# Delta-net trunk: when a background column is added up, where q's square sums are scaled, and what the values and decay products wait for

## The chip, the cores and the metric

The kernel runs on one core of a Trainium2 chip. Its engines work in parallel, each through its own instructions in order: TensorE (PE in the profile) multiplies matrices and transposes through an identity, VectorE (DVE) and ScalarE (ACT) work element by element, GpSimd (POOL) takes small work, SyncE (SP) issues DMAs. Engines wait for each other by semaphores. Matrix products land in PSUM, which this kernel cuts into named tiles of 128x512 floats: four called `acc`, two called `mm` and two called `sc`.

The metric is the device time of one execution, in microseconds (us). Three runs of the kernel before took 2936.68, 2944.91 and 2948.51 us; the median is 2944.91 us.

## The reference

A trunk of two layers over 1024 positions of width 1024. Each layer is a mixer and a gated feed-forward network, both modulated by six vectors per layer that are computed from a conditioning vector `c`. The mixer of layer 0 is a gated delta net with 8 heads, that of layer 1 is retention.

```python
e = jax.nn.silu(c @ cond_w + cond_b)
for i in range(DEPTH):
    mod = (e @ ada_w[i] + ada_b[i])[:, None, :]
    sh1, sc1, g1, sh2, sc2, g2 = jnp.split(mod, 6, axis=-1)
    y = mixers[i % N_MIXERS](x * (1.0 + sc1) + sh1)
    x = layer_norm(DN_ALPHA * x + (1.0 + g1) * y, ln_g[i, 0], ln_b[i, 0])
    y = conv_ffn(x * (1.0 + sc2) + sh2, ffn_up[i], ...)
    x = layer_norm(DN_ALPHA * x + (1.0 + g2) * y, ln_g[i, 1], ln_b[i, 1])
```

The delta net, cut to what the change touches:

```python
qkv = jax.nn.silu(causal_dwconv(qkv, conv_w))
q = _l2norm(q) * (dk ** -0.5)          # divides by sqrt(sum of squares + 1e-6)
k = _l2norm(k)
kk = jnp.where(strict, (k * beta) @ k.T * decay, 0.0)
...                                     # solve with (I + kk), scan over chunks
o = o * lax.rsqrt(jnp.mean(o * o, -1) + 1e-6) * norm_w
```

## The kernel before, in words

The stage that matters is the delta net, about 85 to 645 us of the span. The 8 heads go through it as 4 pairs, numbered 0 to 3. For each pair the kernel runs several Python generators: `t_path` (decay matrices and the inverse of a triangular matrix in 32x32 blocks), `t_chain` (the inverse put together from 32 to 64 to 128 by small matmuls), `prep` (values and keys transposed to PSUM and scaled back by VectorE), `dt_half` (products of keys and queries times the decay), and two `scan`s over 8 chunks with `tail`s that normalize the output. Beside them runs one generator `filler`: the projections of the normalized input onto q, k, v and z, some 30 units of 48 matmuls `acc<-hT` of 128x512 each. The function `run` interleaves all of them into one order for TensorE: it keeps an estimated clock (each matmul has a cost), takes the generator of the lowest priority number that is ready, and lets `filler` go on where nothing else is ready. A generator that yields a number sleeps so long on that clock; one that yields `after_ev(...)` waits for events that others emit, and `emit(name, lat)` sets an event that much after the clock. TensorE keeps exactly this order (`pm` and `ptr` pin each instruction behind the last). The orders of VectorE, ScalarE, GpSimd and the DMA queues are not pinned: a scheduler places each of their instructions from the program and its dependencies.

The steps that are touched, with the lines of the profile:

* **Square sums.** `ssq_tile` transposes a finished q feature to an `acc` tile (L717 `acc<-cst,qkv`), ScalarE squares it chunk by chunk with a running sum (L509), and one VectorE operation on 128x8 numbers adds 1e-6 and scales (L511). It is run once for each of the 8 q features, the first ones before the pairs start. The scaled sums are read only in `tail`, at L1090.
* **Features.** `conv_half` copies a projection out of `acc` (L485, L488), VectorE adds three shifted terms (L490), and ScalarE applies the silu (L491).
* **The 32x32 inverse.** Row by row on VectorE (L883, L885), then VectorE transposes it (L888, `RX`), ScalarE reorders it (L890), VectorE transposes that (L892, `TX`). `t_path` then emits `("Tq", p)` at once, and `("T", p)` 4.98 us later on the estimated clock. `t_chain` waits for `("T", p)`; ScalarE copies blocks of `TX` (L919, six of them) and `RX` (L930, eight) into place before its first matmuls `mm<-T,U`.
* **Values and decay products.** `prep` and `dt_half` wait for `("Tq", p)`. `prep` transposes values to an `mm` tile (L717 `mm<-cst,qkv`), VectorE scales them out of it (L994). `dt_half` multiplies keys and queries into an `mm` tile (L714 `mm<-qkv`), VectorE multiplies by the decay that a DMA has loaded (L1029). There are two `mm` tiles, so a third group on TensorE waits until VectorE has emptied the first.
* **Background columns.** The modulation vectors needed later are computed in the background: `bg_ada` puts 8 units per vector on a list `bg`, and every call of `bg_step` (one per unit of `filler`) takes the next one. A unit loads 256 rows of a matrix (SyncE's queue) and returns its work with a count, which goes on the list `pend` and is run that many calls later: VectorE multiplies and adds into the tile `ada` (L237, L239), of which there is one buffer. After four units TensorE transposes `ada` (L249), ScalarE copies the four blocks back into `ada` with row sums (L251), and VectorE adds the bias (L253, or L255 where no 1 is added). Three vectors, 24 units, are computed during the delta net; `filler` calls `bg_step` 29 times. More are computed in later stages.

TensorE's order around a pair's inverse is: filler matmuls, square sums, `mm<-qkv` and `mm<-cst,qkv` groups mixed with filler, then the 32x32 chain `mm<-T,U`, filler, the 64x64 chain, and the scan.

Of the kernel before, what the change touches and what calls it, by code (L numbers as in the profile page):

```python
# [33 lines left out]
def trunk_kernel(ctx: ExitStack, tc, A):  # L34
# [84 lines left out]
    def bg_step(tile=mm_tile):  # L119
        bg_ps[0] = tile  # L120
        for p in pend:
            p[0] -= 1
        while pend and (pend[0][0] <= 0 or not bg):
            pend.pop(0)[1]()
            if not bg:
                break
        if bg:
            nxt = bg.pop(0)()
            if nxt:
                pend.append(list(nxt))  # L130
# [90 lines left out]
    def bg_ada(i, j, kind):  # L221
# [8 lines left out]
        def work(nh, kp, wr):  # L230
# [3 lines left out]
            for kk in range(2):  # L234
                k = kp * 2 + kk
                if k == 0:
                    dve.tensor_scalar(a, wr[:, 0], e[:, 0:1], None, ALU.mult)  # L237
                else:
                    dve.scalar_tensor_tensor(a, wr[:, kk], e[:, k:k + 1], a, ALU.mult, ALU.add)  # L239
            if kp < KT // 2 - 1:  # L240
                return
            if kind == "col":
# [7 lines left out]
                for g in range(4):  # L250
                    act.activation(a[:, g * P:(g + 1) * P], tp[:, g * P:(g + 1) * P], AF.Copy, accum_out=pt[:, g:g + 1])  # L251
                if j in (1, 2, 4):
                    dve.scalar_tensor_tensor(v, pt, 1.0, b, ALU.add, ALU.add)  # L253
                else:
                    dve.tensor_add(v, pt, b)  # L255
            else:
# [240 lines left out]
    def ssq_tile(ti, tr):  # L497
        o = feats[ti]
        r = ssq[ti] = ct(f"ssq{ti}", [P, NCH])
        for half in range(2):  # L500
            pt = acc_tile()
            sq = tl("cv", [P, 516], name="sq")
            for c in range(4):
                cs = slice(c * P, (c + 1) * P)
                tr(pt[:, cs], o[half][:, cs])
            for c in range(4):
                n = half * 4 + c
                cs = slice(c * P, (c + 1) * P)
                act.activation(sq[:, cs], pt[:, cs], AF.Square, accum_out=r[:, n:n + 1])  # L509
        if ti < GH:  # L510
            dve.tensor_scalar(r, r, 1e-6, 1e-6 * P, ALU.add, ALU.mult)  # L511
        else:
            dve.tensor_scalar(r, r, 1e-6, None, ALU.add)

# [204 lines left out]
    def after_ev(*names):  # L719
        return ("ev", names)  # L720
# [265 lines left out]
    def prep(p):  # L986
        heads = pairs[p]
        yield after_ev(("Tq", p), *[("f", 2 * GH + h) for h in heads])
        for q4 in range(2):
# [17 lines left out]
    def dt_half(p, q4):  # L1007
        heads = pairs[p]
        if q4 == 0:
            yield after_ev(("Tq", p), ("M", p - 1))  # L1010
            yield from take("lane", 1)
            t = tl("lane", [P, 2, HALF], name="DT")
            tiles = [t[:, 0], t[:, 1]]
        else:
            yield after_ev(("Tq", p), ("S", p - 1))
            yield from take("auh", 2)
            emit(("Dt", p))
            tiles = [tl("auh", [P, HALF], name="DT") for _ in range(2)]
# [563 lines left out]

    def layer_tail(i, mix, wout, xsrc, x_mid, x_out, ln_next, final):
        sc2, sh2 = fold(i, 1, 2 * i)
        if i == 0:
# [75 lines left out]
        while rowq or rowp:  # L1661
# [4 lines left out]
                       (gb2, x_out) if final else None, ln_next, "hTb", ("hTb", "hTa", 8, 6, "f") if final else ("qkv", "hTa", 8, 4, "0"), x_out, ("out", i)))  # L1666

    g1 = two("auh", F32, "g1")
    for nh in range(2):
# [353 lines left out]
```

## Time and profile before

| | |
|---|---|
| runs | 2936.68, 2944.91, 2948.51 us; median 2944.91 us |
| the profiled execution: its time | 2944.47 us |
| its span, first to last instruction | 2942.7 us |
| mean granted TensorE clock | 0.983 |
| instructions | 38900 |
| DMA | 459.01 MB, mean 156 GB/s |

How to read the lines of the profile: `L994` is line 994 of the kernel. A line of a timeline has the start in us from the span's start, the length in us, the engine, the line, the operation, what it writes and reads (`out<-in`), the shape, and how many such instructions in a row it stands for; in brackets how long the engine had been idle before and which instruction of which engine it had waited for. Consecutive matmuls are pipelined, so their lengths overlap; the distance of two starts is what one costs. A line of a view of waits has: engine, its instruction, whom it waited for, and the idle time in total, the number of times and the longest in us. A line of a view of windows has the stretch, its length, the busy time of PE, PE's weight loads, DVE, ACT and POOL with instruction counts, the granted TensorE clock as a share of full speed, the DMA share and the rate. In a view of one line of code each row gives the shortest, median and longest duration in ns, and the first and last start.

### The profile page before, as it was taken

The page shows a single profiled execution, that of the slowest core. Times are in us where ns is not written, and L with a number is a line of the kernel's source. Part 1 is how long each engine was busy: PE and PEld are TensorE (multiplying, and loading weights), DVE is VectorE, ACT ScalarE, POOL GpSimd, SP SyncE. Part 2 cuts the span into 40 slices and gives each one's busy share as a digit, 9 for nine tenths or more (in the row PEclk, how much of TensorE's full clock was granted, in tenths as well). Part 3 has the DMA queues.
Part 4 walks back from the last instruction along what each step waited for, and adds up shares of the span by engine and source line. Part 5 has one row for each costly group of instructions (what it writes and reads, how often), then busy time and mean ns, then how long its engine had stood idle before and what let it go on. Part 6 is the DMA issues. An engine that isn't in the chain of part 4 may idle for free. (4 is left out here: it accounts for less than half of the span.)

```text
span 2942.7 us, 38900 instructions
## 1 busy us (share of the span) xinstructions
PE 2815.8 (96%) x13594; PEld 2298.3 (78%) x13594; DVE 2208.4 (75%) x3976; ACT 1314.9 (45%) x2413; POOL 497.8 (17%) x517
## 2 busy tenths in 40 slices
PE   8999899999999999999999999999999899999997
PEld 6887777887778888887778877777777788888886
DVE  6878788656688888868686665566689787777779
ACT  4745564444544444545333333222344544444543
POOL 0312221100013332200000021422202023331001
PEclk9999899999999999999999999999999999999999
DMA  7231222243255655755333364655663253334753
GB/s 279 80 119 62 80 79 80 83 167 137 93 176 175 208 189 188 270 185 184 132 136 115 129 231 145 208 171 170 194 231 131 102 165 133 135 126 162 291 184 115
DMA packets 248276, 459.01 MB, mean 156 GB/s; under 512 B 23632, under 2 KB 77264, under 8 KB 248080
## 3 DMA queue, kind: packets, MB, share of 16 engines
q1 hardware_dynamic: 215680, 404.87, 40.9%
q10 hardware_dynamic: 29760, 43.00, 4.0%
q0 software_dynamic: 2640, 8.65, 0.8%
q8 instruction: 107, 1.75, 0.2%
q14 instruction: 89, 0.73, 0.1%
HBM read 343.71 MB, written 112.72 MB: 155 GB/s over the span
## 5 line engine op out<-in xcount | busy, mean ns | idle before, releaser
L714 PE MATMUL acc<-hT,wh 128*128 128x512 f32 x960 | 301.3, 395 | 0.0
L1504 PE MATMUL acc<-bb,ab 128*128 128x512 f32 x984 | 236.2, 398 | 10.9 <-DVE bb L90 9.3
L1504 PEld LDWEIGHTS acc<-bb,ab 128*128 128x128 f32 x984 | 186.0, 191 | 55.2 <-DVE bb L90 14.2
L714 PEld LDWEIGHTS acc<-hT,wh 128*128 128x128 f32 x960 | 183.4, 191 | 34.5
L1229 PE MATMUL acc<-T,wb 128*128 128x512 f32 x840 | 203.6, 391 | 6.9 <-DVE wb L90 6.8
L89 ACT ACTIVATE ab<-ar 128x512 fp32r<-128x512 f32 x210 | 130.2, 626 | 171.2 <-PE mm L303 46.9
L714 PE MATMUL acc<-hT,wl 128*128 128x512 f32 x480 | 202.3, 421 | 0.0
L411 POOL TENSOR_TENSOR xg<-xg,gb 128x512 f32<-128x512 f32 x48 | 62.4, 1302 | 773.6 <-DMA xg<-xs 761.4
L1229 PEld LDWEIGHTS acc<-T,wb 128*128 128x128 f32 x840 | 156.5, 188 | 45.0 <-DVE wb L90 10.4
L90 DVE TENSOR_TENSOR ab<-ar,ab 128x512 fp32r<-128x512 f32 x210 | 147.5, 708 | 57.6 <-ACT ab L89 57.6
L90 DVE TENSOR_TENSOR wl<-wr,wh 128x1024 fp32r<-128x1024 f32 x98 | 123.0, 1256 | 86.9 <-ACT wh L89 86.7
L1654 POOL TENSOR_TENSOR o<-o 128x512 f32<-128x512 f32 x80 | 124.7, 1568 | 288.8 <-ACT pc L1290 190.1
L90 DVE TENSOR_TENSOR wb<-wr,wb 128x512 fp32r<-128x512 f32 x162 | 116.9, 726 | 71.6 <-ACT wb L89 69.4
L89 ACT ACTIVATE wh<-wr 128x1024 fp32r<-128x1024 f32 x98 | 103.9, 1062 | 143.5 <-PE acc L714 70.5
L90 DVE TENSOR_TENSOR wb<-mm,wb 128x512 fp32r<-128x512 f32 x216 | 145.8, 683 | 27.5 <-ACT wb L89 26.8
L1633 DVE SCALAR_TENSOR_TENSOR o<-g,vc,o 128x512 f32<-128x512 f32 (+2 forms) x176 | 155.0, 897 | 5.3 <-ACT o L1628 4.6
L89 ACT ACTIVATE wb<-mm 128x512 fp32r<-128x512 f32 x216 | 124.0, 595 | 64.4 <-DVE mm L1279 61.3
L1290 ACT ACTIVATE pc<-acc 128x512 f32<-128x512 f32 x143 | 84.6, 592 | 144.2 <-PE acc L1229 88.5
L89 ACT ACTIVATE wb<-wr 128x512 fp32r<-128x512 f32 x162 | 98.6, 627 | 107.6 <-DMA wr<-in_ffn_up 50.2
L714 PE MATMUL acc<-wh,hT 128*128 128x512 f32 x384 | 135.2, 416 | 1.0 <-DVE vv L90 1.0
L110 PE MATMUL acc<-T,wb 128*128 128x512 f32 x292 | 116.0, 397 | 9.4 <-DVE wb L90 9.4
L490 DVE SCALAR_TENSOR_TENSOR qkv<-raw,vc,qkv 128x512 f32<-128x512 f32 x144 | 110.3, 769 | 14.2 <-ACT qkv L488 13.5
(651 smaller groups left out, 7456.4 us busy)
## 6 DMA issues: line engine op xcount, KB each, us to landing
wr<-in_ffn_up SPq DMA_DIRECT2D x92, 512.0 KB, 4.3
mvw<-in_ada_w SPq DMA_DIRECT2D x80, 512.0 KB, 4.4
ad<-o SPq DMA_DIRECT2D x154, 256.0 KB, 3.1
ar<-ad SPq DMA_DIRECT2D x154, 256.0 KB, 3.8
Br<-in_ffn_down SPq DMA_DIRECT2D x88, 256.0 KB, 3.4
wr<-in_ret_wv SPq DMA_DIRECT2D x32, 512.0 KB, 4.2
ar<-od SPq DMA_DIRECT2D x56, 256.0 KB, 4.9
wr<-in_gdn_wqkv SPq DMA_DIRECT2D x24, 512.0 KB, 3.5
```

Source lines behind the costliest of these rows:

```text
L89: act.activation(dst_h, src, AF.Copy)
L90: eng.tensor_tensor(dst_l, src, dst_h, ALU.subtract)
L110: mm(acc, wl[:, k], hl[0], start=first, stop=False)
L411: pool.tensor_tensor(x, x, gb[0], ALU.mult)
L490: dve.scalar_tensor_tensor(oh, raw[:, 3 - j:515 - j], w[:, 3 - j:4 - j], oh, ALU.mult, ALU.add)
L714: pq(pe.matmul(out, lhsT, rhs, start=start, stop=stop), cost)
L1229: return pe.matmul(*a, skip_group_check=True, **kw)
L1290: act.activation(t, X, AF.Copy)
L1504: return pe.matmul(*args, skip_group_check=True, **kw)
L1633: dve.scalar_tensor_tensor(tv, gv[:, c0 - j:c1 - j], w[:, 2 - j:3 - j], tv, ALU.mult, ALU.add)
L1654: (dve if fp == 0 else pool).tensor_tensor(o[d], o[x], o[y], op)
```

## The change

Three things are done, and two loops added that empty the background lists.

1. The last addition of a background column (L253, L255) is not issued with ScalarE's sums but put on `pend` with the count 2, so that it is issued two calls of `bg_step` later, behind the multiplication of the next unit in program order (`after("ada")`). `bg_step` now runs every entry of `pend` whose count is up, not only entries at the head of the list. Before the rows of layer 0's gain and at the start of `layer_tail` the lists are emptied.
2. The scaling of the square sums (L511, once for each q feature on 128x8 numbers) is taken out of `ssq_tile`; `tail` scales its own half (16 times on 128x4).
3. `prep` and both halves of `dt_half` wait for `("T", p)` in place of `("Tq", p)`.

```diff
@@ bg_step
-        while pend and (pend[0][0] <= 0 or not bg):
-            pend.pop(0)[1]()
-            if not bg:
-                break
+        ready = [p for p in pend if p[0] <= 0] or ([] if bg else pend[:1])
+        for p in ready:
+            pend.remove(p)
+            p[1]()
@@ bg_ada, work
-                    dve.tensor_scalar(a, wr[:, 0], e[:, 0:1], None, ALU.mult)
+                    anchor["ada"] = dve.tensor_scalar(a, wr[:, 0], e[:, 0:1], None, ALU.mult)
                 else:
-                    dve.scalar_tensor_tensor(a, wr[:, kk], e[:, k:k + 1], a, ALU.mult, ALU.add)
+                    anchor["ada"] = dve.scalar_tensor_tensor(a, wr[:, kk], e[:, k:k + 1], a, ALU.mult, ALU.add)
...
-                if j in (1, 2, 4):
-                    dve.scalar_tensor_tensor(v, pt, 1.0, b, ALU.add, ALU.add)
-                else:
-                    dve.tensor_add(v, pt, b)
+                def fin():
+                    with after("ada"):
+                        if j in (1, 2, 4):
+                            dve.scalar_tensor_tensor(v, pt, 1.0, b, ALU.add, ALU.add)
+                        else:
+                            dve.tensor_add(v, pt, b)
+
+                pend.append([2, fin])
@@ ssq_tile
-        if ti < GH:
-            dve.tensor_scalar(r, r, 1e-6, 1e-6 * P, ALU.add, ALU.mult)
-        else:
-            dve.tensor_scalar(r, r, 1e-6, None, ALU.add)
@@ prep
-        yield after_ev(("Tq", p), *[("f", 2 * GH + h) for h in heads])
+        yield after_ev(("T", p), *[("f", 2 * GH + h) for h in heads])
@@ dt_half
-            yield after_ev(("Tq", p), ("M", p - 1))
+            yield after_ev(("T", p), ("M", p - 1))
...
-            yield after_ev(("Tq", p), ("S", p - 1))
+            yield after_ev(("T", p), ("S", p - 1))
@@ tail
         act.activation(d, o, AF.Square)
+        dve.tensor_scalar(ssq[h][:, qs], ssq[h][:, qs], 1e-6, 1e-6 * P, ALU.add, ALU.mult)
         dve.tensor_reduce(so, d, AX.X, ALU.add)
@@ layer_tail, and before the rows of g1
+        while bg or pend:
+            bg_step()
```

The changed lines shift what follows: L237 and L239 keep their numbers, L253 and L255 become L255 and L257, L485 to L491 become L489 to L495, L509 becomes L513, L714 and L717 become L715 and L718, L919 and L930 become L920 and L931, L994 becomes L995, L1029 becomes L1030, and the new scaling in `tail` is L1090.

More of the change, by code (lines that the diff above doesn't have):

```diff
@@ L1666, in layer_tail @@
                        (gb2, x_out) if final else None, ln_next, "hTb", ("hTb", "hTa", 8, 6, "f") if final else ("qkv", "hTa", 8, 4, "0"), x_out, ("out", i)))
+    while bg or pend:
+        bg_step()
     g1 = two("auh", F32, "g1")
```

## The prediction

> **What bounds the kernel now.** The page's first part comes first: which engine has no slack.
>
> ```profile
> PE 2815.8 (96%) x13594; PEld 2298.3 (78%) x13594; DVE 2208.4 (75%) x3976; ACT 1314.9 (45%) x2413; POOL 497.8 (17%) x517
> ```
>
> TensorE is busy for 2815.8 of 2942.7 us, and the change leaves its instructions the same in number. So it can gain only where TensorE idles or runs at a lower clock. Next, the views of what TensorE and VectorE wait for, cut to the edited lines:
>
> ```profile
> PE mm L714 <- DVE qkv L994: 10.2, 4, 4.2
> PE mm L717 <- DVE DT L1029: 5.7, 3, 2.5
> DVE ssq L511 <- ACT sq L509: 13.2, 6, 5.0
> DVE v L253 <- ACT ada L251: 10.9, 7, 2.5
> DVE v L255 <- ACT ada L251: 9.3, 4, 4.0
> ```
>
> TensorE loses 10.2 + 5.7 = 15.9 us to L994 and L1029, which empty the two `mm` tiles. VectorE loses time to the three lines that are moved. The timelines show that these are the same places. TensorE:
>
> ```profile
> 204.25 0.66 PE L717 MATMUL mm<-cst,qkv 128*128 128x128 f32 x4 [1.68 <-DVE DT L1029]
> ...
> 306.50 0.66 PE L717 MATMUL mm<-cst,qkv 128*128 128x128 f32 x4 [1.57 <-DVE DT L1029]
> ...
> 315.31 0.71 PE L714 MATMUL mm<-gm,m_lowr 128*128 128x512 f32 x2 [1.93 <-DVE qkv L994]
> ...
> 319.21 2.98 PE L714 MATMUL mm<-T,U 32*32 32x32 f32 x56 [2.50 <-DVE qkv L994]
> ...
> 439.78 0.94 PE L714 MATMUL mm<-qkv 128*128 128x128 f32 x6 [1.63 <-DVE qkv L994]
> ...
> 443.42 0.66 PE L717 MATMUL mm<-cst,qkv 128*128 128x128 f32 x4 [2.48 <-DVE DT L1029]
> ...
> 564.11 1.22 PE L714 MATMUL mm<-qkv 128*128 128x128 f32 x4 [4.15 <-DVE qkv L994]
> ```
>
> VectorE, just ahead of each:
>
> ```profile
> 202.22 0.16 DVE L253 SCALAR_TENSOR_TENSOR v<-cs,vc 128x4 f32<-128x4 f32 x1 [2.52 <-ACT ada L251]
> ...
> 305.68 0.17 DVE L511 TENSOR_SCALAR ssq<-ssq 128x8 f32<-128x8 f32 x1 [0.79 <-ACT sq L509]
> 305.75 1.45 DVE L1029 TENSOR_TENSOR DT<-DT,mm 128x512 f32<-128x512 f32 x2
> ...
> 314.40 0.16 DVE L255 TENSOR_TENSOR v<-cs,vc 128x4 f32<-128x4 f32 x1 [4.05 <-ACT ada L251]
> 314.48 0.68 DVE L994 TENSOR_TENSOR qkv<-mm,ir 128x512 f32<-128x512 f32 x1
> ...
> 438.96 0.17 DVE L511 TENSOR_SCALAR ssq<-ssq 128x8 f32<-128x8 f32 x1 [5.03 <-ACT sq L509]
> ...
> 563.29 0.17 DVE L511 TENSOR_SCALAR ssq<-ssq 128x8 f32<-128x8 f32 x1 [4.62 <-ACT sq L509]
> ```
>
> A tiny VectorE operation waits for ScalarE, L994 and L1029 stand queued behind it, and both `mm` tiles stay full. The seven idle times add up to 15.9. ScalarE is late because the copies of the inverse stand ahead of its sums:
>
> ```profile
> 305.49 3.48 ACT L930 ACTIVATE R<-RX 32x128 f32<-32x128 f32 x8
> 308.99 4.09 ACT L919 ACTIVATE T<-TX 32x256 f32<-32x256 f32 x6
> 313.10 0.28 ACT L251 ACTIVATE ada<-acc 128x128 f32<-128x128 f32 x1
> ...
> 314.25 0.60 ACT L485 ACTIVATE raw<-acc 128x512 f32<-128x512 f32 x1
> 314.72 0.70 ACT L488 ACTIVATE qkv<-acc,vc 128x512 f32<-128x512 f32 x1
> ...
> 432.04 0.63 ACT L491 ACTIVATE qkv<-qkv 128x512 f32<-128x512 f32 x1
> 432.57 4.05 ACT L919 ACTIVATE T<-TX 32x256 f32<-32x256 f32 x6
> ...
> 550.91 0.62 ACT L491 ACTIVATE qkv<-qkv 128x512 f32<-128x512 f32 x1
> ...
> 556.98 3.98 ACT L919 ACTIVATE T<-TX 32x256 f32<-32x256 f32 x6
> ```
>
> Three of these waits have a second price. In the view of windows the share behind PE's, PEld's, DVE's, ACT's and POOL's busy times is the granted clock:
>
> ```profile
> 319.00:335.00 16.00, 15.79 (x181) 13.35 (x182) 10.95 (x22) 6.38 (x8) 4.36 (x6) 0.51 0.34 108
> 444.00:448.00 4.00, 4.00 (x20) 3.71 (x20) 1.92 (x4) 0.63 (x1) 0.00 (x0) 0.57 0.29 112
> 448.00:460.00 12.00, 12.00 (x199) 10.11 (x198) 6.48 (x11) 5.33 (x7) 4.64 (x6) 1.00 0.01 2
> 564.00:570.00 6.00, 5.89 (x20) 5.21 (x21) 2.27 (x6) 1.83 (x5) 0.00 (x0) 0.50 0.03 11
> 895.00:1210.00 315.00, 313.01 (x1384) 255.83 (x1383) 273.54 (x417) 152.09 (x312) 88.71 (x72) 1.00 0.57 193
> ```
>
> After the waits of pairs 1, 2 and 3 TensorE runs at about half clock. What that costs is the stretch by the missing share: 16 x 0.49 = 7.8, 4 x 0.43 = 1.7 and 6 x 0.50 = 3.0 us, together 12.5. The small matmuls of the chain do not do it by themselves: in 448 to 460 pair 2's chain runs at 1.00.
>
> **The change part by part.** What the edits are worth hangs on where the build puts the moved instructions, so I read the changed kernel's own instruction order on each engine beside these rows.
>
> *The last additions.* L255 and L257 no longer wait. But the tile `ada` has one buffer, and L237, the next unit's first multiplication, must wait for the same L251. In VectorE's new order L237 stands ahead of L995 and L1030 in each pair with such a column, with the addition right behind it. The wait has a new owner. It is shorter only where ScalarE's L251 comes sooner. In the feed-forward network the 7 waits of L253 and L255 pass to L237 too; TensorE there is busy 313.01 of 315 us (the last row above), so that is worth nothing; without that cover it would be at most 10.9 + 9.3 less the 2.52 and 4.05 shown, 13.6 us, and the same in both kernels.
>
> *The square sums.* All 16 new scalings stand in VectorE's order where L511 stood, not at the tails: the scheduler may lift them, since their input is ready. The wait for ScalarE's L513 stays. The eight operations more are 8 x 0.17 = 1.4 us of VectorE, which is idle for a quarter of the time: nothing on the path; 1.4 us at most.
>
> *Values and decay products after the inverse.* This is what really moves work. Their transposes and products on TensorE come 12 to 24 filler matmuls later, mixed into the 32x32 chain; so do the loads of L1022 on SP's queue (whose data no instruction of this stage was seen waiting for) and L995 and L1030 on VectorE. The wait for the square sums then has filler on TensorE to cover it. The price: ScalarE's silu of the next q feature (L495) now stands behind the copies of the inverse in pairs 2 and 3, and TensorE's second square-sum transposes wait for it.
>
> Pair 0: the 1.68 at 204.25 goes, since the products come after filler: gain 1.7 (bounds 0 and 1.7).
>
> ```profile
> L237 DVE TENSOR_SCALAR ada<-mvw,e x20: 477/480/487, 69.6 to 2382.3; 128x512 f32<-128x512 f32 x20
> ```
>
> Pair 1: ScalarE's new order is three L931, L489, L492, two L931, four L251, six L920. From 305.49 that is 5 x 0.435 (3.48 / 8) for the L931, 0.47 + 0.6 for L489 and L492 (the distance of L485 and L488 above, and L488 nearly whole), and 1.2 for the four L251 (313.10 to 314.25): it ends at 310.0 to 310.1, not 314.25. L237 (0.48 by the row above), one L239 and one L1030 (about 0.7 each, as L994 and L1029 in their rows) follow: the tile is free at about 311.9. TensorE reaches that wait about 309.7 (after 303.9, when it starts on pair 1's products before, it now has 18 filler matmuls and four groups to do), so it idles 2.2 us there and, group by group behind the next L1030, L995 and L828, 1.6 more: 3.8. The other bound is the 6.00 of before (1.57 + 1.93 + 2.50) with one L1030 and one L239 more (0.7 each), 7.4. I take the middle, 5.5. The half clock is the larger term: nearest to several microseconds of idle in groups is the 4.15 of pair 3, which cost 3.0; bounds 0 and the 7.8 measured here. Before 6.0 + 7.8 = 13.8, after 5.5 + 3.0 = 8.5: gain 5.3 (bounds -1.4 and 10.0).
>
> Pair 2. Before, the silu came ahead of the six copies and TensorE waited little:
>
> ```profile
> 432.72 0.66 PE L717 MATMUL acc<-cst,qkv 128*128 128x128 f32 x4 [0.23 <-ACT qkv L491]
> 554.69 1.04 PE L717 MATMUL acc<-cst,qkv 128*128 128x128 f32 x8
> ```
>
> Behind the 4.05 of copies the wait becomes 4.3. Removed are 1.63 + 2.48 + 1.7 = 5.8. With the half clock of the 4.15 wait (3.0) the new sum is 7.3: loss 1.5 (bounds: gain 1.5 without it, loss 6.3 with 7.8).
>
> Pair 3: the second row above shows no wait before. Now the silu starts after the copies, which end at 560.96 before and about 3 us sooner after, since the feature's L494s and a weight split no longer stand between the rows of the inverse; it ends near 558.6, and TensorE is there at 555.4 (554.69 with three filler matmuls more and a group less). New wait 3.2, up to 6.2 if the inverse is no sooner. Removed are 4.15 + 3.0 = 7.15. A wait of 3.2 lies between 2.48 (price 1.7) and 4.15 (3.0); I take 2.3. Gain 1.7 (bounds 4.0 and -6.9).
>
> End of the scan: three scan steps now stand without projection matmuls between them.
>
> ```profile
> 642.19 0.50 PE L326 MATMUL acc<-wh,hl 128*128 128x512 f32 x1 [0.83 <-DVE hl L90]
> 644.76 0.49 PE L714 MATMUL acc<-w,DT 128*128 128x128 f32 x2 [0.46 <-ACT w L1057]
> ```
>
> By these rows that costs 0 to 2 us; I take 1. ScalarE gets two more loads of its function table in pair 1:
>
> ```profile
> L491 ACT ACT_TABLE_LOAD x7: 1283/1283/1283, 89.0 to 467.8; - x7
> ```
>
> 2.6 us on an engine that is 45% busy: nothing, or 2.6 if on the chain.
>
> Sum: 1.7 + 5.3 - 1.5 + 1.7 - 1 = 6.2 us. The profiled execution took 2944.47 us, 0.4 below the median of the runs; 2944.5 - 6.2 gives 2938 us.
>
> **The rivals.** *A: all waits vanish.* If the filler covers ScalarE's lateness everywhere, the gain is 15.9 + 12.5 = 28.4: 2916. For it: every wait removed is short. Against it: L237 and L1090 inherit them in VectorE's order, and the silu is a new one.
>
> *B: short half clock.* If the half clock after each new wait is that of 444 to 448 us, 1.7, and none after 3.2: 1.7 + (13.8 - 5.5 - 1.7) + (5.8 - 4.3 - 1.7) + (7.15 - 3.2) - 1 = 11.0, so 2933. For it: the 2.48 of pair 2. Against it: the 16 us after pair 1's 2.50. [...]
>
> *C: the change does not do what it says.* Waits only get new owners and the clock falls as often: -1 to +3 around no gain, 2944.
>
> *D: slower.* The silu behind the copies decides. If each new wait is followed by a half clock as long as pair 1's (7.8), pair 1 loses 1.4 with its idle at 7.4, pair 2 loses 6.3, pair 3 loses 3.9, the end 1, and pair 0 gains 1.7: 10.9 slower, 2955; with pair 3's wait at 6.2, 2958. It begins to decide when half clock after the waits of pairs 1 to 3 exceeds some 14.5 us in sum, 8.3 of it being in the forecast.
>
> **How the numbers follow.** Forecast 0.36 (its own range 2930 to 2946), A 0.16, B 0.16, C 0.10, D 0.22. From one run to the next the shown times differ by up to 0.4%, so about 0.5%, 14.7 us, can be told from no change. Faster than 2930: A with 0.16, and 0.08 from B and the lower end of the forecast, 0.24. Slower than 2960: half of D, 0.11. The rest, 0.65, lies between. The range 2920 to 2957 leaves out most of A and the upper part of D, about 2 in 10.
>
> **What would show it.** L237 at L251's waits, at 310 and not 314 us; L1090 where L511 stood, near 305, 439 and 563; a wait of TensorE's square-sum transposes for L495 of some 4.3 in pair 2 and 3.2 in pair 3; granted clock over 0.8 through pair 1's 32x32 chain. The sum is wrong if L995 and L1030 do not hold TensorE in pair 1, if no half clock follows the silu waits, or if the scan or the later stages differ by more than 2 us.

## The result, and the profile after

The changed kernel takes 2950.14 us (median of 22 runs, 2940.48 to 2962.97), the kernel before 2943.84 us beside it (22 runs, 2936.11 to 2953.45). The ratio is 1.0022 with a 95% interval of 1.0013 to 1.0032: 6.3 us slower. That is inside the 0.5% that the forecast called no change, and inside its range; but the forecast's own sum was 6.2 us faster, so its sign is wrong.

The page of the changed kernel, its first lines and engine totals:

```profile
span 2948.0 us, 38912 instructions
...
PE 2815.7 (96%) x13594; PEld 2296.1 (78%) x13594; DVE 2211.8 (75%) x3984; ACT 1316.7 (45%) x2415; POOL 499.8 (17%) x517
```

TensorE's busy time, which has the longer time of matmuls at half clock in it (two filler matmuls take 0.85 us at 394.31 us, at half clock, and 0.46 at 397.19, at full), is the same to 0.1 us. So the 5.3 us that the span has more are idle time of TensorE; 2.6 us of it lie in the stage below (43.4 against 40.8 us). What TensorE and VectorE wait for (engine, instruction, whom; total, times, longest in us):

```profile
PE acc L718 <- ACT qkv L495: 6.8, 2, 3.8
PE mm L718 <- DVE DT L1030: 4.4, 3, 2.7
PE mm L715 <- DVE R L963: 4.3, 4, 2.0
...
PE mm L715 <- DVE DT L1030: 1.8, 3, 0.7
...
PE mm L715 <- DVE qkv L995: 0.5, 1, 0.5
...
DVE ada L237 <- ACT ada L251: 21.5, 8, 9.1
...
DVE ssq L1090 <- ACT sq L513: 14.9, 9, 7.8
```

The 15.9 us of waits for L994 and L1029 are down to 6.7 (4.4 + 1.8 + 0.5). But 6.8 us of waits for the silu and 4.3 us for L963 (the chain's own results) are new, and VectorE still waits as long as before in sum: L237 has the wait of L253 and L255 (21.5 us for 20.2), L1090 that of L511 (14.9 for 13.2). In the delta net L237 waits only once, 9.13 us in pair 0; its other seven waits, of 1.76 us each, are in the feed-forward network. In pair 1, where L255 waited 4.05 us until 314.40, L237 starts at 310.43 without a wait. TensorE's timeline, the waits that answer to the seven of before:

```profile
210.36 0.66 PE L718 MATMUL mm<-cst,qkv 128*128 128x128 f32 x4 [2.71 <-DVE DT L1030]
...
312.96 0.66 PE L718 MATMUL mm<-cst,qkv 128*128 128x128 f32 x4 [1.06 <-DVE DT L1030]
...
329.20 1.19 PE L715 MATMUL mm<-gm,m_lowr 128*128 128x512 f32 x2 [1.96 <-DVE R L963]
...
437.25 0.88 PE L718 MATMUL acc<-cst,qkv 128*128 128x128 f32 x4 [3.76 <-ACT qkv L495]
...
564.25 1.12 PE L718 MATMUL acc<-cst,qkv 128*128 128x128 f32 x4 [3.07 <-ACT qkv L495]
```

The first is the surprise of pair 0. VectorE's timeline there, and ScalarE's instruction that it waits for:

```profile
201.29 0.49 DVE L237 TENSOR_SCALAR ada<-mvw,e 128x512 f32<-128x512 f32 x1 [9.13 <-ACT ada L251]
...
204.51 0.69 DVE L995 TENSOR_TENSOR qkv<-mm,ir 128x512 f32<-128x512 f32 x1 [0.34 <-PE mm L718]
207.21 1.23 DVE L90 TENSOR_TENSOR wl<-wr,wh 128x1024 fp32r<-128x1024 f32 x1 [2.01 <-ACT wh L89]
208.96 0.75 DVE L239 SCALAR_TENSOR_TENSOR ada<-mvw,e,ada 128x512 f32<-128x512 f32 x1 [0.53 <-DMA mvw<-in_ada_w]
209.63 1.28 DVE L1030 TENSOR_TENSOR DT<-DT,mm 128x512 f32<-128x512 f32 x2
...
206.12 1.06 ACT L89 ACTIVATE wh<-wr 128x1024 fp32r<-128x1024 f32 x1 [1.45 <-DMA wr<-in_gdn_wqkv]
```

L237's 9.13 us cost nothing, since no product is waiting yet. But the products now come late enough to stand behind the weight split of the next filler unit (L90). That waits for L89, and L89 for a load that lands at 206.1. L1030 starts at 209.63 only, and both `mm` tiles are full.

The second surprise is not one row. The stage runs from pair 0's `RX` to the last weight load of L326 (L330 in the changed kernel), just before the output projection ends, and is cut at the first 64x64 matmul of each pair. In the view of windows a row has stretch, length, PE busy, PEld, DVE, ACT, POOL and granted clock. Of the kernel before, then of the changed one:

```profile
224.37:337.27 112.90, 100.40 (x694) 85.34 (x693) 86.75 (x242) 58.33 (x136) 25.10 (x39) 0.86 0.20 68
337.27:464.30 127.03, 116.49 (x820) 98.76 (x819) 101.56 (x267) 70.98 (x157) 28.73 (x43) 0.99 0.21 70
464.30:582.40 118.10, 108.93 (x779) 93.80 (x778) 90.18 (x251) 62.74 (x151) 15.87 (x29) 0.96 0.26 91
...
642.19:745.80 103.61, 97.73 (x442) 79.62 (x443) 71.82 (x122) 44.45 (x62) 4.92 (x6) 0.97 0.46 157
...
385.00:400.00 15.00, 12.74 (x79) 10.90 (x78) 14.11 (x38) 7.48 (x15) 0.37 (x1) 1.00 0.22 71
```

```profile
226.69:335.80 109.11, 96.93 (x696) 81.38 (x695) 86.89 (x247) 60.27 (x139) 26.02 (x39) 0.92 0.21 71
335.80:466.60 130.80, 118.74 (x811) 100.45 (x810) 98.90 (x265) 69.51 (x155) 28.43 (x43) 0.95 0.20 65
466.60:587.71 121.11, 112.23 (x791) 95.88 (x791) 91.09 (x253) 63.42 (x153) 16.98 (x27) 0.96 0.27 90
...
648.98:750.50 101.52, 97.56 (x436) 79.66 (x437) 70.23 (x119) 42.35 (x58) 4.92 (x6) 0.95 0.46 156
...
385.00:400.00 15.00, 12.30 (x63) 10.62 (x62) 11.81 (x32) 6.73 (x14) 0.31 (x1) 0.77 0.22 70
```

Length less PE busy is idle; length times the missing clock is what half clock can cost at most. Pair 1's stretch has its clock back (112.90 x 0.14 = 15.8 us before, 109.11 x 0.08 = 8.7 after). But the next stretch loses 130.80 x 0.05 = 6.5 where it lost 1.3, half of it at 385 to 400 us, in pair 1's scan.

Each kernel was profiled three times (the two repeats are the last runs of the list of experiments below). The lengths of the stretches in us, executions 1, 2, 3, and their means:

| stretch | before | mean | after | mean | difference |
|---|---|---|---|---|---|
| to pair 0's 64x64 | 36.3, 37.5, 36.4 | 36.7 | 38.6, 39.1, 39.3 | 39.0 | +2.3 |
| to pair 1's | 112.9, 111.2, 107.2 | 110.4 | 109.1, 104.4, 104.3 | 105.9 | -4.5 |
| to pair 2's | 127.0, 127.0, 128.1 | 127.4 | 130.8, 129.4, 129.5 | 129.9 | +2.5 |
| to pair 3's | 118.1, 118.1, 117.0 | 117.7 | 121.1, 121.2, 121.2 | 121.2 | +3.5 |
| to the output projection | 59.8, 60.0, 60.0 | 59.9 | 61.3, 61.4, 61.4 | 61.4 | +1.5 |
| output projection | 103.6, 103.7, 104.7 | 104.0 | 101.5, 103.0, 103.0 | 102.5 | -1.5 |
| PE idle in all | 40.8, 42.3, 40.5 | 41.2 | 43.4, 43.9, 43.6 | 43.6 | +2.4 |

The stage is 3.7 us longer. What the median has beyond that (2.6 us) lies within the scatter of the rest of the kernel, which these six profiles do not resolve.

### The profile page after: what moved, and what is told of

Read it like the earlier page. It is cut to its first block, busy times and chain, and to the rows that moved or that the text cites. A ratio compares the mean times of both kernels' runs of the same rounds, so it can differ in the third digit from the quotient of the medians.

```text
span 2948.0 us, 38912 instructions
## 1 busy us (share of the span) xinstructions
PE 2815.7 (96%) x13594; PEld 2296.1 (78%) x13594; DVE 2211.8 (75%) x3984; ACT 1316.7 (45%) x2415; POOL 499.8 (17%) x517
## 5 line engine op out<-in xcount | busy, mean ns | idle before, releaser
L715 PE MATMUL acc<-hT,wh 128*128 128x512 f32 x960 | 303.5, 398 | 0.0
L1506 PE MATMUL acc<-bb,ab 128*128 128x512 f32 x984 | 233.0, 394 | 11.8 <-DVE bb L90 10.2
L715 PEld LDWEIGHTS acc<-hT,wh 128*128 128x128 f32 x960 | 185.2, 193 | 35.4
L89 ACT ACTIVATE ab<-ar 128x512 fp32r<-128x512 f32 x210 | 130.3, 626 | 170.3 <-PE mm L307 46.2
L715 PE MATMUL acc<-hT,wl 128*128 128x512 f32 x480 | 203.3, 424 | 0.7 <-ACT sq L513 0.7
L1231 PEld LDWEIGHTS acc<-T,wb 128*128 128x128 f32 x840 | 157.8, 189 | 46.3 <-DVE wb L90 10.5
L90 DVE TENSOR_TENSOR ab<-ar,ab 128x512 fp32r<-128x512 f32 x210 | 146.1, 701 | 58.3 <-ACT ab L89 58.3
L90 DVE TENSOR_TENSOR wl<-wr,wh 128x1024 fp32r<-128x1024 f32 x98 | 122.9, 1255 | 85.0 <-ACT wh L89 84.9
L90 DVE TENSOR_TENSOR wb<-wr,wb 128x512 fp32r<-128x512 f32 x162 | 114.8, 713 | 70.2 <-ACT wb L89 70.2
L90 DVE TENSOR_TENSOR wb<-mm,wb 128x512 fp32r<-128x512 f32 x216 | 145.7, 683 | 27.5 <-ACT wb L89 26.7
L89 ACT ACTIVATE wh<-wr 128x1024 fp32r<-128x1024 f32 x98 | 103.9, 1061 | 127.0 <-PE acc L715 61.0
L89 ACT ACTIVATE wb<-mm 128x512 fp32r<-128x512 f32 x216 | 124.0, 595 | 64.3 <-DVE mm L1281 61.0
L89 ACT ACTIVATE wb<-wr 128x512 fp32r<-128x512 f32 x162 | 98.4, 627 | 108.2 <-DMA wr<-in_ffn_up 49.3
L715 PE MATMUL acc<-wh,hT 128*128 128x512 f32 x384 | 135.0, 415 | 1.0 <-DVE vv L90 1.0
L110 PE MATMUL acc<-T,wb 128*128 128x512 f32 x292 | 115.9, 397 | 9.6 <-DVE wb L90 9.6
```

The lines of the kernel that those rows point to most:

```text
L89: act.activation(dst_h, src, AF.Copy)
L90: eng.tensor_tensor(dst_l, src, dst_h, ALU.subtract)
L110: mm(acc, wl[:, k], hl[0], start=first, stop=False)
L715: pq(pe.matmul(out, lhsT, rhs, start=start, stop=stop), cost)
L1231: return pe.matmul(*a, skip_group_check=True, **kw)
L1506: return pe.matmul(*args, skip_group_check=True, **kw)
```

## The experiments

Each ratio is to the kernel before on the same chip, with its 95% interval. The last two columns are the wait of TensorE's second square-sum transposes for the silu in pairs 2 and 3, where it is over 0.5 us.

| kernel | ratio | pair 2 | pair 3 |
|---|---|---|---|
| whole change | 1.0022 [1.0013, 1.0032] | 3.76 | 3.07 |
| part three only | 1.0015 [1.0000, 1.0030] | 3.77 | 3.06 |
| part one only | 0.9999 [0.9987, 1.0012] | | |
| part two only | 0.9995 [0.9982, 1.0009] | | |
| parts one and two, ada twice, sums bound | 1.0069 [1.0046, 1.0092] | | 2.20 |
| part three, values only | 1.0060 [1.0045, 1.0075] | 3.72 | 2.66 |
| part three, products only | 0.9991 [0.9975, 1.0007] | | |
| part three, all copies behind the silu | 1.0009 [0.9998, 1.0021] | 0.84 | |
| part three, half the delay | 0.9988 [0.9976, 0.9999] | | 3.04 |
| part three, pair 0 only | 0.9993 [0.9981, 1.0006] | | 3.23 |
| part three, pair 1 only | 1.0025 [1.0014, 1.0036] | 3.78 | 2.65 |
| part three, pairs 2 and 3 only | 1.0011 [1.0000, 1.0022] | | 2.66 |
| whole, half the delay, sums bound | 1.0005 [0.9992, 1.0017] | | |
| whole, silu first in pair 2 | 1.0002 [0.9988, 1.0016] | | |
| part three for pair 1, silu first in pair 2 | 1.0000 [0.9985, 1.0014] | 1.49 | |

**The three parts, one at a time.** The theory was that part three alone costs the time, the rivals that one of the others does.

```diff
-        yield after_ev(("Tq", p), *[("f", 2 * GH + h) for h in heads])
+        yield after_ev(("T", p), *[("f", 2 * GH + h) for h in heads])
...
-            yield after_ev(("Tq", p), ("M", p - 1))
+            yield after_ev(("T", p), ("M", p - 1))
```

> Only the third part of the change: the values and the decay products wait for the event T; the additions and the scaling stay as before. Theory (the moved events are what costs: the weight split ahead of L1029 in pair 0 and the silu behind the copies of the inverse in pairs 2 and 3): as slow as the whole change, 4 to 8 us slower than before, the delta net's end 5 to 7 us later than in the kernel before (642.19 us), with TensorE's two silu waits of 3 to 4 us. Rival (the deferred additions or the scalings make VectorE late): within 2 us of before, and no silu waits.

Median 2948.82 against 2943.76 us, 5.1 us slower; the interval just reaches no change. The waits of TensorE, with the lines of before:

```profile
PE acc L717 <- ACT qkv L491: 6.8, 2, 3.8
PE mm L717 <- DVE DT L1029: 4.1, 3, 2.7
```

The silu waits and pair 0's 2.7 us are those of the whole change. The stage's end came at 642.00 us, not 5 to 7 us later as expected: this one execution took 2945.77 us, 3 less than its kernel's median, and its windows show little half clock (11.8 us in the stage by their clocks, against a mean of 22.6 before).

Part one alone keeps the other two as before:

```diff
-                if j in (1, 2, 4):
-                    dve.scalar_tensor_tensor(v, pt, 1.0, b, ALU.add, ALU.add)
-                else:
-                    dve.tensor_add(v, pt, b)
+                def fin():
+                    with after("ada"):
+                        ...
+                pend.append([2, fin])
```

> Only the first part: the last additions of the background columns come two calls later, and the lists are emptied at the end. Theory (the wait for ScalarE's sums only passes from L253 and L255 to L237): within 2 us of before; L237 waits for L251 some 20 us in sum, 7 or 8 times; TensorE's 15.9 us of waits for L994 and L1029 stay. Rival (this part gains what it was meant to and the events give it back): 3 to 6 us faster, TensorE's waits in pairs 0 and 1 gone.

```profile
DVE ada L237 <- ACT ada L251: 19.9, 10, 4.0
```

The wait of L253 and L255 (20.2 us before) is L237's now. TensorE's waits for the two `mm` tiles stay (14.7 us), and the time is the same.

Part two alone:

```diff
-        if ti < GH:
-            dve.tensor_scalar(r, r, 1e-6, 1e-6 * P, ALU.add, ALU.mult)
...
+        dve.tensor_scalar(ssq[h][:, qs], ssq[h][:, qs], 1e-6, 1e-6 * P, ALU.add, ALU.mult)
```

> Only the second part: the square sums are scaled in the tail. Theory (the scheduler lifts the scalings to where L511 stood): within 2 us of before, the 16 scalings near 305, 439 and 563 us with 13 us of waits for ScalarE's squares. Rival (they stand at the tails): the waits of 1.6 and 4.2 us of TensorE in pairs 2 and 3 gone, 5 to 9 us faster.

```profile
L1086 DVE TENSOR_SCALAR ssq<-ssq x16: 130/170/943, 104.1 to 560.3; 128x4 f32<-128x4 f32 x16
...
DVE ssq L1086 <- ACT sq L509: 13.5, 10, 4.9
```

All 16 scalings (L1086 in this kernel) are issued between 104.1 and 560.3 us, before the last tails, and wait 13.5 us, where L511 waited 13.2. Neither part one nor part two shows a gain or a loss by itself, within intervals of some 0.13% each way; part three has the loss.

**What parts one and two mean to do.** Two buffers, and a scaling that cannot be lifted, with the events as before:

```diff
-"ada": 1,
+"ada": 2,
...
-        dve.scalar_tensor_tensor(so, so, 1.0 / P, ssq[h][:, qs], ALU.mult, ALU.add)
+        dve.tensor_scalar(so, so, 1.0 / P, 1e-12 * P, ALU.mult, ALU.add)
+        dve.scalar_tensor_tensor(so, ssq[h][:, qs], 1e-6 * P, so, ALU.mult, ALU.add)
```

> What parts one and two mean to do, without part three: two buffers for ada, so that the next unit's multiplication waits for nothing; the scaling of the square sums made from the tail's own sum, (so/P + 1e-12 P) + ssq * 1e-6 P, so that it can't be issued before it; values and decay products wait for Tq as before. Theory (the waits of TensorE before come from ScalarE's sums through VectorE's queue and can be taken away): TensorE's waits for L994 and L1029 fall from 15.9 to under 8 us, and the time by 5 to 15 us. Rival (ScalarE's late copies hold TensorE anyway, at the chain's start): the waits pass to the 32x32 chain or to the silu, and the time stays within 3 us of before.

Neither: 1.0069. TensorE's waits for L995 and L1030 are 12.9 us, not under 8, and a silu wait of 2.20 us is new. The delta net ended at 640.69 us, but the loss is in the feed-forward network. The window of 900 to 1500 us, of this kernel and of the one before:

```profile
900.00:1500.00 600.00, 573.14 (x2516) 464.41 (x2516) 471.64 (x740) 278.91 (x526) 100.21 (x83) 0.99 0.55 187
```

```profile
900.00:1500.00 600.00, 590.37 (x2612) 482.46 (x2611) 483.91 (x765) 288.08 (x542) 111.64 (x83) 0.99 0.55 188
```

TensorE idles 27 instead of 10 us there. Over the whole kernel VectorE's background multiplications now wait for their loads, 19.9 us at L237 and 13.4 at L239 against 0.7 and 8.8 before, and TensorE's waits for the splits L90 at L110 rise from 9.4 to 15.3 us. That the second buffer puts these multiplications ahead of the splits is likely, but it was not tried apart. A run further below, with the sums bound and one buffer, does not lose this time (1.0005).

**Which of the moved groups.** Values alone, products alone, and the order of silu and copies turned round:

```diff
# values only: only prep waits for T; products only: only dt_half
...
# copies behind the silu
-        act.activation(oh, oh, AF.Silu)
+        anchor["silu"] = act.activation(oh, oh, AF.Silu)
...
+                with after("silu"):
                     act.activation(T0[bs, hh, :, cs], TX[bs, :, ch]...)
```

> Part three for the values alone: prep waits for T, the decay products for Tq as before. In the built order the products of pair 0 stand ahead of the weight split again, and the silu stands behind the copies of the inverse in pairs 2 and 3. Theory (the silu waits are the larger cost): 3 to 6 us slower than before, TensorE's two silu waits of 3 to 4 us there, the 2.7 us of pair 0 gone. Rival (the weight split ahead of the products in pair 0 is the cost): within 2 us of before.

Slower as the theory said, but by 18 us and not 3 to 6. The waits of TensorE there:

```profile
PE mm L714 <- DVE R L962: 6.8, 4, 2.4
PE acc L717 <- ACT qkv L491: 6.4, 2, 3.7
PE mm L714 <- DVE qkv L994: 3.7, 1, 3.7
```

Pair 0's wait is gone, so the weight split is not needed for a loss. Idle in the stage is 52.2 us, 11 more than before: values moved without the products also hold up the chain. Why so much is open.

> Part three for the decay products alone: both halves of dt_half wait for T, prep for Tq. In the built order the weight split stands ahead of the products in pair 0 (as in the whole change), and the silu ahead of the copies in pairs 2 and 3 (as before). Theory (silu): within 2 us of before, no silu wait over 1 us, a wait of 2 to 3 us for L1029 in pair 0. Rival (weight split): 3 to 6 us slower.

Within the theory's bounds (0.9991), with the wait in pair 0 that it named (2.4 us), though also with waits of 3.25 us in pair 1 and 4.87 us in pair 2 that nobody expected. The first and the last of them:

```profile
211.54 0.66 PE L717 MATMUL mm<-cst,qkv 128*128 128x128 f32 x4 [2.44 <-DVE DT L1029]
...
446.14 1.19 PE L714 MATMUL mm<-gm,m_lowr 128*128 128x512 f32 x2 [4.87 <-DVE DT L1029]
```

> Part three whole, and ScalarE's copies of the inverse (L919, L930) queued behind the last silu issued before them. Theory (silu): TensorE's silu waits fall under 1 us each, and the time to within 2 us of before; the 2.7 us of pair 0 stay. Rival (the silu's time is on loan: the copies, later by a silu and the squares, hold the 32x32 chain instead): the chain's first matmuls wait 3 us or more in pairs 2 and 3, and the time stays 4 to 8 us above before.

1.0009: between the two, and its interval holds both. The silu waits fall to 0.84 us, but others take their place, in kind as the rival had it: for the 32x32 chain's copies (`xa`), though 2.35 us in pair 1 and 1.54 in pair 2 and not 3 in pairs 2 and 3, and 4.07 us for pair 3's squares:

```profile
PE acc L714 <- ACT sq L509: 4.7, 2, 4.1
...
PE mm L717 <- ACT xa L947: 4.3, 4, 2.3
```

> Part three with half the delay: values and products wait for an event 2.5 us after Tq on the estimated clock, T being 4.98 us after. In the built order the products of pair 0 stand ahead of the split, and the silu behind the copies in pair 3 only. Theory (silu): 1 to 3 us slower than before, with one silu wait of about 3 us. Rival (what counts is that the groups stand later at all, in proportion): half of the loss of part three, 2 to 3 us slower, without it showing in one wait.

```diff
+        emit(("Th", p), 2.5)
...
-        yield after_ev(("Tq", p), *[("f", 2 * GH + h) for h in heads])
+        yield after_ev(("Th", p), *[("f", 2 * GH + h) for h in heads])
```

Neither: 0.9988, the fastest of all. Pair 3's silu wait is there (3.04 us) and the time is not longer. So the theory was too wide: in this execution pair 3's wait takes the place of the 4.15 us that were there before.

**Pair by pair.**

```diff
-        yield after_ev(("Tq", p), ...)
+        yield after_ev(("T" if p in (0,) else "Tq", p), ...)
```

> Part three for pair 0 alone (values and decay products of pairs 1 to 3 wait for Tq as before). In the built order pair 0's products stand behind the weight split; pair 3's silu also slips behind the copies, as the scheduler's own times shift. Theory (each pair has its own price, and pair 0's is the weight split, whose data comes late from the load): the stretch from pair 0's inverse to its 64x64 chain 2 to 3 us longer than the 36.3 to 37.5 of before, with one wait of 2.5 to 3 us for L1029; in all 1 to 4 us slower. Rival (the split is hidden by filler, and pair 0's longer stretch comes back in pair 1): the stretches of pairs 0 and 1 together as long as before, the time within 1.5 us.

The price is there, in the first row, and in pair 3 the silu wait, in the second:

```profile
210.67 0.66 PE L717 MATMUL mm<-cst,qkv 128*128 128x128 f32 x4 [2.75 <-DVE DT L1029]
...
561.41 0.66 PE L717 MATMUL acc<-cst,qkv 128*128 128x128 f32 x4 [3.23 <-ACT qkv L491]
```

Pair 0's stretch is 40.2 us, 2.7 more than the longest of before. Yet the time is not longer (0.9993): the stretch to pair 3 took 114.5 us against 117.0 to 118.1. The theory's price is right for the place and wrong for the whole. The rival does not fit either: the stretches of pairs 0 and 1 together are 152.0 us, against 143.6 to 149.2 before.

> Part three for pair 1 alone. In the built order the silu also slips behind the copies in pairs 2 and 3. Theory: pair 1's stretch (64x64 chain to 64x64 chain) 3 to 6 us shorter than the 107.2 to 112.9 of before, pairs 2 and 3 together 2 to 6 us longer through two silu waits of 3 to 4 us; in all within 3 us of before. Rival (pair 1's gain is a chance of the clock): its stretch within 2 us of before, and the time 2 to 6 us slower.

Pair 1's stretch is 108.6 us, inside the 107.2 to 112.9 of before: no gain in this execution. Pairs 2 and 3 together take 253.1 us against 245.1, 245.1 and 245.1 (127.0 + 118.1, 127.0 + 118.1, 128.1 + 117.0). The time is as long as that of the whole change, although pairs 2 and 3 have their old events. The silu has slipped behind the copies there too, although only pair 1's groups were moved:

```profile
432.06 0.66 PE L717 MATMUL acc<-cst,qkv 128*128 128x128 f32 x4 [3.78 <-ACT qkv L491]
...
562.01 0.66 PE L717 MATMUL acc<-cst,qkv 128*128 128x128 f32 x4 [2.65 <-ACT qkv L491]
```

The time fits the rival better. But in this one execution the loss does not lie at pair 2's wait. The stretches of pairs 2 and 3:

```profile
333.26:457.09 123.83, 113.52 (x808) 96.02 (x807) 99.28 (x263) 70.48 (x155) 29.16 (x43) 0.99 0.21 69
457.09:586.34 129.25, 117.99 (x798) 99.58 (x797) 90.98 (x251) 64.68 (x154) 16.92 (x29) 0.92 0.24 82
```

Pair 2's stretch is 3.2 us shorter than in the first execution of before, with 12 filler matmuls fewer (2.7 us); it is idle for 10.3 us against 10.5, and its clock is 0.99 in both. The silu wait takes the place of most of the waits for L994 and L1029 there. Pair 3's stretch is the longer one: 18 filler matmuls more (4.1 us), 11.3 us idle against 9.2, and a clock of 0.92 against 0.96.

> Part three for pairs 2 and 3 alone. In the built order pair 2 keeps its silu ahead of the copies, pair 3's stands behind. Theory: one silu wait of about 3 us in pair 3, pairs 0 and 1 as before, the time 0 to 4 us slower than before. Rival (the later values and products cost as such, whichever wait shows): 4 to 8 us slower.

1.0011, within the theory's bounds; pair 2 keeps its silu ahead in this order.

> The whole change with two corrections: values and products wait for an event 2.5 us after Tq in place of 4.98, and the scaling of the square sums is made from the tail's own sum, so that no VectorE operation waits for ScalarE's squares ahead of the products. In the built order the products of pair 0 stand ahead of the split, and the silu ahead of the copies in every pair. Theory (the intentions are sound where the order carries them out): no silu wait over 1 us, TensorE's waits for L995 and L1030 under 12 us together, and 4 to 12 us faster than before, faster than both kernels. Rival (TensorE waits for the inverse itself, and only the place of the wait moves): within 3 us of before.

The rival holds: 1.0005. No silu wait is left, and TensorE idles 40.3 us in the stage, against 40.5 to 42.3 before. TensorE waits for L1031 for 7.0 us, and in pair 3 for the squares instead:

```profile
PE mm L718 <- DVE DT L1031: 7.0, 4, 4.0
...
PE acc L715 <- ACT sq L513: 3.0, 2, 2.8
```

**The silu of pair 2 alone.** By now the four kernels with the pair 2 wait had ratios of 1.0015 to 1.0060, and the others, but for the one with two ada buffers, 0.9988 to 1.0011. All four have pair 3's wait as well; three of the others have pair 3's alone (0.9988, 0.9993, 1.0011). The last two runs move that silu, in the whole change and in the kernel of pair 1:

```diff
-        act.activation(oh, oh, AF.Silu)
+        anchor["silu", tile_idx, half] = act.activation(oh, oh, AF.Silu)
...
+                with after(("silu", 2 * p + 1, 1) if p in (2,) else None):
                     act.activation(T0[bs, hh, :, cs], TX[bs, :, ch]...)
```

> The whole change, with the six copies of TX in pair 2 alone queued behind the silu of the second half of q feature 5, as they stand before. In the built order pair 3's silu then stands ahead of its copies by itself; everything up to pair 2 is as in the whole change. Theory (the silu that slips behind the copies in pair 2 costs what is lost): the two silu waits fall from 6.8 us to under 1, and of the 6.3 us that the whole change loses at least 4 come back, to within 2.5 us of before. Rival (the wait only moves on, to the copies or the squares): still 4 to 8 us slower than before.

> Part three for pair 1 alone (7.4 us slower by its own run, 1.0025), with the copies in pair 2 queued behind the silu as in the run beside it. In the built order the silu stands ahead of the copies in pairs 2 and 3. Theory: pair 1's shorter stretch is kept and the silu waits go, 1 to 6 us faster than before. Rival: still 4 to 8 us slower than before.

Whole change: 2945.49 against 2944.82 us, 1.0002 where it was 1.0022. Pair 1: 1.0000 where it was 1.0025. In both the loss is gone, within the intervals; the second did not become faster than before, which the theory had, and keeps a silu wait of 1.49 us in pair 2. ScalarE and TensorE of the whole change with the silu first, in pair 2, and what came in pair 3:

```profile
430.97 0.63 ACT L495 ACTIVATE qkv<-qkv 128x512 f32<-128x512 f32 x1
431.50 4.10 ACT L921 ACTIVATE T<-TX 32x256 f32<-32x256 f32 x6
...
431.06 1.25 PE L718 MATMUL acc<-cst,qkv 128*128 128x128 f32 x8
...
564.23 0.80 PE L715 MATMUL acc<-hT,wl 128*128 128x512 f32 x1 [5.08 <-ACT sq L513]
```

The eight transposes run without a wait, and the stretch to pair 2's 64x64 chain is 125.7 us, against 129.4 to 130.8 in the changed kernel. In pair 3 a wait of 5.08 us for the squares has taken the place of the silu's 3.07, and the stretch there is 123.5 us against 121.2. So the waits do move on, and by the medians the time still came back. Where it came back the trace does not show: this profiled execution took 2951.54 us, 6 more than its kernel's median, and its stage is 561.4 us long and idle for 44.4, against means of 559.9 and 43.6 in the changed kernel.

**The same kernels again.**

> The kernel before, profiled once more. Theory (half clock is set by how TensorE's idle times fall against windows that run by themselves, and differs between executions): TensorE's waits for L994 and L1029 come back within 0.3 us each and its idle time between pair 0's inverse and the end of the output projection within 2 us of 40.8, but the time lost to half clock there (25.6 us before) moves by 5 us or more in at least one of the two repeats. Rival (half clock belongs to the kernel): within 2 us of 25.6.

> The kernel before, profiled a third time: the same waits and idle time as in the first, by the theory another half clock, by the rival the same.

> The changed kernel, profiled once more. Theory: the two silu waits (3.8 and 3.1 us) and pair 0's 2.7 us come back within 0.3 us, idle time in the same stretch within 2 us of 43.4, and half clock moves by 5 us or more from its 25.6 in at least one repeat. Rival: half clock within 2 us.

> The changed kernel, profiled a third time: the same waits and idle time as in the first, by the theory another half clock, by the rival the same.

The silu waits and pair 0's came back within 0.2 us, the idle totals within 1.5 (the table above); one wait for L994 of before did not, the total was 9.2 instead of 10.2. Half clock moved: pair 1's stretch of the kernel before lost at most 15.8, 12.2 and 8.6 us to it by its windows' clocks (0.86, 0.89, 0.92 of 112.9, 111.2 and 107.2 us). The time lost in the whole stretch moved by 5.1 us in one repeat of before and in both of after, just over the 5 of the theory. But the place is not chance throughout: the clock at 385 to 400 us is 1.00 in all three executions of before and 0.77 in all three of after.

## Why the prediction was wrong

*What bounds the kernel* held: TensorE's busy time did not change, and the part of the difference that is resolved, 3.7 us, lies in the stage from pair 0's inverse to the output projection.

*The last additions and the square sums* held: new owners for the same waits, no gain by themselves (0.9999 and 0.9995). That L237 and L1090 inherit them is what happened in sum. In pair 1 the wait itself is gone, since ScalarE's sums come sooner there, as the forecast had it (L237 at 310.43).

*Pair 0, "gain 1.7": wrong in sign, a loss of 2.3 us at its place.* The step counted the wait of before as covered by filler. Filler did cover it, but the products then stood behind the weight split, which hangs on a load. The built order showed L90 there; the forecast did not ask what L90 waits for. By the run of pair 0 alone, this did not decide the total.

*Pair 1, "gain 5.3": close.* The stretch is 4.5 us shorter, 5.2 with the three filler matmuls more that now stand before its end (0.23 each). Idle there was 12.5, 13.2 and 12.3 us and is 12.2, 12.8 and 12.7; the gain is all clock. At 310 to 340 us, where the forecast looked, half clock went from 8.4, 8.4 and 5.1 us to 5.1, 1.8 and 1.8, by 4.4 in the mean where 4.8 were taken. At 225 to 250 us, which it did not price, it went from 6.8, 3.5 and 3.5 us to 3.5, 0 and 0. In the run of pair 1 alone the clock at these two places is 0.83 and 0.86, as in the third execution of before, so part of the gain may be luck.

*Pair 2, "loss 1.5".* The mechanism was found: the wait was put at 4.3 us and is 3.76, its half clock at 3.0. The windows of the changed kernel after it:

```profile
436.00:440.00 4.00, 2.75 (x9) 2.33 (x10) 0.34 (x2) 3.98 (x20) 0.41 (x3) 0.69 0.34 129
440.00:444.00 4.00, 4.00 (x17) 3.22 (x16) 2.98 (x4) 1.83 (x3) 0.00 (x0) 0.88 0.00 0
```

That is 4 x 0.31 + 4 x 0.12 = 1.7 us, one short stretch at half clock, as rival B had it: the trace records a clock of 0.50 for 3.41 us from 437.55 us, and half of that is 1.7. What failed is the credit beside it: 5.8 us were taken off as removed, but 0.65 and 0.69 us for L1030 and 1.00 for L963 came in their stead, and this stretch has more half clock than before (6.5, 5.2 and 5.2 us against 1.3, 1.3 and 3.8). About 3.4 us of it lie at 385 to 400 us, in pair 1's scan, in all three executions, and none before: a term that the forecast put at nothing. The stretch is 2.5 us longer although 9 filler matmuls (2.1 us) left it, so some 4.6 us are lost where 1.5 were forecast.

*Pair 3, "gain 1.7".* The silu wait was put at 3.2 and is 3.07; the half clock after it was put at 2.3 and is 1.6 (0.73 from 564 to 570 us). The stretch is 3.5 us longer; 2.7 of that are 12 filler matmuls that moved into it and are missing later, so 0.8 us are lost, not 1.7 gained. The 4.15 us taken off came back as small waits: idle was 9.2, 8.2 and 8.4 us and is 8.9, 9.1 and 8.9.

*End of the scan, "1 us": right*, 1.0 us more idle (61.4 - 59.4 = 2.0 against 1.0).

In sum: the forecast had TensorE's idle time 2 us lower (15.9 removed, 5.5 + 4.3 + 3.2 + 1 added) and half clock 4.2 lower. Measured are 2.4 us more idle and, by the windows' clocks, no change in half clock (means 22.6 before, 22.3 after). The step that failed is the one that booked a removed wait and its half clock as gain. Of the 15.9 us of waits, 6.7 stay at L995 and L1030, and 6.8 for the silu and 4.1 more for the chain's L963 stand beside them. Half clock fell by 7.9 us in pair 1's stretch (means 12.2 and 4.3), but rose by 3.5 in pair 2's, by 3.7 in the output projection and by 1.0 up to pair 0's chain.

The medians turn on rival D's mechanism, the silu behind the copies, though by 6 and not by 11 us and without the long half clock that D put beside it. The two runs that put the silu first again recover 0.20% and 0.25%, with 0.17% and 0.18% each way by an estimate from the two intervals of each. That it is pair 2's silu is argued, not shown: both runs take pair 3's silu wait away too, and that this one costs little rests on the three kernels that have it alone. No trace here shows the price of pair 2's wait beyond its own 3.76 + 1.7 us, and in the run of pair 1 alone its stretch was not longer. The 2.6 us that the medians have beyond the stage stay open.

*The rivals:* A fell, since the silu is a new wait. C is what parts one and two did, but not the whole. B's short half clock held in pair 2, its sum did not; that none follows a wait of 3.2 no run had shown, and the runs show both: in pair 3, 1.6 us came with the 3.07 of the changed kernel, but after the 3.06 of part three alone two filler matmuls take 0.46 us (at 559.36), as at full clock.

## What to carry to other kernels

When work on the bounding engine is made later, look in the built order at what it now stands behind on each engine that serves it, and follow each of those to the load or activation it waits for: here a weight split and a silu. Removed waits are not gain until the work that was to fill them is named; across these kernels TensorE idled 39 to 45 us in this stage in whatever order (52 in one). Moving one group can reorder pairs that were not touched, so read the whole order, and pin the one instruction that matters.

## What was not expected of the hardware

Half clock came at waits shorter than the 2.48 us of pair 2, the shortest that the forecast gave a price by itself: in the changed kernel the scan steps at 385 to 400 us wait 1.80 us until 388.46 and 0.90 until 390.73, the trace records a clock of 0.50 from 389.76 to 396.59, TensorE is busy for 12.30 of 15 us, and the clock over them is 0.77. The kernel before has the wait of 1.80 us there too and one of 0.46, is busy for 12.74, and stays at 1.00.

In this stage the traces record half clock as 0.50 and for whole multiples of 3.41 us: in the kernel before 17.1 us from 317.7 us, 3.4 from 444.0 and 6.8 from 563.5. All such records of a trace begin on one grid of 3.4133 us, 0.27 us beyond whole steps from the span's start in the kernel before and 0.64 in the changed one. So what it costs at most moves in steps of 1.7 us; the forecast's windows cover only part of the first and the last, and it put 7.8 and 3.0 us where the records give 8.5 and 3.4.

And the same program differed from execution to execution: 0.86, 0.89 and 0.92 over one stretch of some 110 us, and 2935 to 2956 us in its runs.
